# A state-space layer's outputs in another order of matmuls, and its kernels made four pairs at a time

## The chip, the cores and the metric

One of the eight cores of a Trainium2 chip. The metric is the device time of one execution in microseconds, taken by the hardware profiler; of several runs the median counts.

## What is computed

The reference is four layers in a row on 1024 tokens of width 1024: dilated attention, a grouped state-space layer (S5), and two hybrid layers (short convolution, retention, neighbourhood attention). The change lies in the state-space layer alone:

```python
def s5_scan(u, a_re, a_im, log_dt, b_re, b_im, c_re, c_im, d_skip):
    ...
    a_bar = jnp.exp(A * dt)
    b_bar = ((a_bar - 1.0) / A)[..., None] * Bm
    bu = jnp.einsum('bsgc,gpc->bsgp', uf.astype(jnp.complex64), b_bar)
    ...
    _, states = lax.associative_scan(combine, (a_elems, bu), axis=1)
    y = jnp.einsum('bsgp,gcp->bsgc', states, Cm).real
    y = y + d_skip.astype(f).reshape(SSM_N_GROUPS, SSM_GROUP) * uf
```

There are 64 groups `g` of 16 channels `c`, each with 64 complex states `p`.

## The kernel before

Everything is f32, or f32 split into a high and a low part that are multiplied in three matmuls of 128x512 (`mm3`, L168). These projections fill most of TensorE's (PE's) time. Smaller work is cut into jobs, which a counter of matmuls (`tick`, `pace`) lets in between the projections when the program is written down; after that the compiler's scheduler orders each engine's instructions by its own model of when they are ready.

The state-space layer works on 8 blocks of four pairs of groups (index `k` for the pair, `g` for the group within it; the two groups' states lie on partitions 0 to 63 and 64 to 127). Time is cut into 128 chunks of 8 steps. Within a chunk a short kernel is applied directly; across chunks the states are scanned.

*Tables* (`ssm_setup`, during attention). For each block, `ca` makes the matrix that takes states to outputs, `wj` the one that takes inputs to states, and `kmat` (L798 to L819) the kernel within a chunk: for each of the four pairs two products, for the real and the imaginary part, of a 128x32 operand `u_bd` (both groups of the pair side by side, filled by POOL at L805) with a 128x128 slice of `u_A`. All eight go to partitions 0 to 31 of one PSUM bank, at column 128k (L812). DVE copies them out and adds the skip term on the diagonal (L815, L816), and two DMAs store them.

*The layer itself* (`ssm`, `core`). Each block goes through jobs: `load`; `inject` (L905, inputs to state increments, 64 columns of PE at a time); `demod`, `scan`, `remod` on DVE with help of POOL (L916 to L948), which leave the states `S` as a real and an imaginary tile; `outputs(0)` and `outputs(1)`, one per group; `turn`, which transposes the outputs (L969, L970). `outputs(g)` takes one PSUM tile `T` of a pool of two, and for each pair `k` issues three matmuls that accumulate onto the same 128 columns: inputs by kernel (L956, all 128 partitions as contraction), then real and imaginary states by `ca` (L958, 64 partitions, those of group `g`). ACT then applies gelu to each pair (L963).

`together` (L128) issues a list of matmuls and binds all but the first to be queued behind the first; attention uses it for its last products (L132 is the first matmul of a list, L135 the rest).

An f32 matmul leaves two records each of weight load and matmul in the trace. In a row of PE, `64*128 64x128` means a weight of 64 partitions by 128 columns and a moving operand of 64x128.

Of the kernel before, what the change touches and what calls it, by code (L numbers as in the profile page):

```python
# [75 lines left out]
class Ker:  # L76
# [534 lines left out]
    def ssm_setup(self, p):  # L611
# [14 lines left out]
        def room(tag, shape):  # L626

            return p.tile(shape, F32, name=self.uid(tag), tag=tag, bufs=1)
# [21 lines left out]
        def load():  # L650
# [5 lines left out]
            d = p.tile([32, 32], F32, name="u_d", tag="u_d", bufs=1)  # L656
            nc.sync.dma_start(d, A["s_d"])
            t_["d"] = d
            e = p.tile([32, 16], F32, name="u_eye", tag="u_eye", bufs=1)
            V.tensor_tensor(e, self.ident[0:32, 0:16], self.ident[0:32, 16:32], op=ALU.add)  # L660
            t_["eye"] = e
# [136 lines left out]
        def kmat(b):  # L798

            o = t_["ca"].rearrange("p i n j c -> p i n (j c)")  # L800
            kt = room("u_C", [32, 4, 128])
            for i, bb in enumerate(("br", "bi")):
                for g in range(2):
                    r = slice(64 * g, 64 * g + 64)
                    G.tensor_copy(t_["bd"][r, i, :, 16 * g:16 * g + 16], t_[bb][r, b * 4:b * 4 + 4])  # L805
            dd = p.tile([32, 4, 16], F32, tag="u_dd", name=self.uid("u_dd"), bufs=1)
            V.tensor_tensor(dd, t_["eye"].unsqueeze(1).to_broadcast([32, 4, 16]),
                            t_["d"][:, b * 4:b * 4 + 4].unsqueeze(2).to_broadcast([32, 4, 16]), op=ALU.mult)
            ps = self.pt()
            for k in range(4):  # L810
                for i in range(2):
                    nc.tensor.matmul(ps[0:32, k * 128:(k + 1) * 128], t_["bd"][:, i, k], o[:, i, k, 0:128],  # L812
                                     start=i == 0, stop=i == 1)
            pv = ps[0:32].rearrange("p (k n) -> p k n", n=128)
            V.tensor_copy(kt[:, :, 16:128], pv[:, :, 16:128])  # L815
            V.tensor_tensor(kt[:, :, 0:16], pv[:, :, 0:16], dd, op=ALU.add)  # L816
            kd = self.kd[b].rearrange("(k g) c x -> g c k x", g=2)
            for g in range(2):
                nc.sync.dma_start(kd[g, :, :, 128:256], kt[16 * g:16 * g + 16])  # L819
# [42 lines left out]
    def ssm(self, x_src, x_dst, mod, ctx=None):  # L862
# [5 lines left out]
        with ExitStack() as es:  # L868
# [14 lines left out]
            def core(b):  # L883
# [67 lines left out]
                def outputs(g):  # L951
                    ps = self.pt()
                    r = slice(64 * g, 64 * g + 64)
                    for k in range(4):
                        o = ps[:, k * 128:k * 128 + 128]
                        nc.tensor.matmul(o, L["u"][:, 2 * k + g], L["m"][:, 2 * k + g], start=True, stop=False)  # L956
                        for i in range(2):
                            nc.tensor.matmul(o, L["S"][i][r, k], L["ca"][r, i, k], start=False, stop=i == 1)  # L958
                    if g == 0:
                        L["y"] = p.tile([128, 8, 128], F32, tag="y", name=self.uid("y"), bufs=1)  # L960
                    yo = L["y"].rearrange("p i (k g c) -> p g k i c", g=2, c=16)[:, g]
                    for k in range(4):
                        ACT.activation(yo[:, k], ps[:, k * 128:k * 128 + 128].rearrange("p (i c) -> p i c", c=16),  # L963
                                       AF.Gelu_apprx_tanh)
# [8 lines left out]
                return [load, inject, demod, scan, remod, lambda: outputs(0), lambda: outputs(1),  # L973
# [1013 lines left out]
def extras(inp):  # L1987
# [13 lines left out]
    e["s_d"] = np.ascontiguousarray(inp["ssm_d"][0].reshape(32, 32).T)  # L2001
# [61 lines left out]
```

## Time and profile before

| | us |
|---|---|
| runs: median (lowest, highest) of 3 | 3279.22 (3279.18, 3291.76) |
| profiled execution | 3278.89 |
| its span, first to last instruction | 3276.3 |
| PE busy in the span | 3156.0 |
| mean granted TensorE clock, share of full | 0.988 |

The trace shows each instruction's engine, source line, operands, start and duration. A matmul's duration contains a tail in which the next one already runs, so PE's pace is read from one start to the next. Stretches are given in us from the start of the span: 147 to 415 holds the kernels of all eight blocks (and attention's first part), 1390 to 1615 the layer's blocks.

### The profile page before, as it was taken

The numbers are of one execution on the slowest core, as the hardware profiler recorded it, in microseconds if no ns is written. First come the engines' busy times: TensorE is split into PE (matmuls) and PEld (weight loads), VectorE is DVE, ScalarE is ACT, GpSimd is POOL, SyncE is SP. The second block draws the span as 40 slices with busy tenths as digits, with TensorE's granted clock in tenths as the row PEclk, the third lists the DMA queues.
The fourth block names the chain that finished last, engine by engine and source line by source line (L and its number), as shares of the span: only waits on it lengthen the run. The fifth ranks groups of instructions, "written<-read, shape, count | busy, mean of one in ns | idle before, by whom it ended". The sixth has DMA issues, their size and how long they took to land. (4 is left out here: it accounts for less than half of the span.)

```text
span 3276.3 us, 48205 instructions
## 1 busy us (share of the span) xinstructions
PE 3156.0 (96%) x18340; PEld 2605.9 (80%) x18340; DVE 1931.2 (59%) x4147; ACT 1212.1 (37%) x2498; POOL 589.9 (18%) x769
## 2 busy tenths in 40 slices
PE   7999999999999999999999999999999999999998
PEld 6888787877788787778788888777887888778777
DVE  5565668777866647655544734445457754555455
ACT  4544444444444454322332121134443212234351
POOL 1244402121111101111002122210002212210001
PEclk9999999999999999999999999999999999999999
DMA  4223233333322225555433211132215322133232
GB/s 136 60 71 101 72 94 107 90 94 91 105 70 81 73 82 172 183 157 148 122 122 116 73 52 51 51 103 83 77 58 174 107 65 65 46 98 89 69 115 97
DMA packets 325242, 312.86 MB, mean 95 GB/s; under 512 B 27833, under 2 KB 277396, under 8 KB 325012
## 3 DMA queue, kind: packets, MB, share of 16 engines
q1 hardware_dynamic: 325012, 309.80, 31.2%
q8 instruction: 144, 2.36, 0.3%
q14 instruction: 86, 0.70, 0.1%
HBM read 249.64 MB, written 60.09 MB: 95 GB/s over the span
## 5 line engine op out<-in xcount | busy, mean ns | idle before, releaser
L168 PE MATMUL mm<-aTh,wh 128*128 128x512 f32 (+1 forms) x2704 | 1076.1, 398 | 29.2 <-DVE qk L353 8.2
L168 PE MATMUL mm<-aTl,wh 128*128 128x512 f32 (+1 forms) x2704 | 1073.6, 397 | 0.9 <-DVE aTl L221 0.6
L168 PE MATMUL mm<-aTh,wl 128*128 128x512 f32 (+1 forms) x2704 | 1070.0, 396 | 0.6 <-DVE wl L155 0.6
L168 PEld LDWEIGHTS mm<-aTh,wh 128*128 128x128 f32 x2704 | 513.6, 190 | 137.6 <-issue 6.9
L168 PEld LDWEIGHTS mm<-aTh,wl 128*128 128x128 f32 x2704 | 513.6, 190 | 102.7 <-issue 2.9
L168 PEld LDWEIGHTS mm<-aTl,wh 128*128 128x128 f32 x2704 | 513.4, 190 | 102.0 <-issue 4.8
L155 DVE TENSOR_TENSOR wl<-wr,wh 128x1024 fp32r<-128x1024 f32 x176 | 225.4, 1281 | 191.4 <-ACT wh L154 190.9
L154 ACT ACTIVATE wh<-wr 128x1024 fp32r<-128x1024 f32 x176 | 186.0, 1057 | 381.8 <-PE mm L168 329.5
L414 ACT ACTIVATE sb<-sb,st 128x128 f32<-128x128 f32 (+1 forms) x384 | 170.3, 444 | 268.1 <-DVE st L412 266.9
L168 PE MATMUL mm<-wo,aTh 128*128 128x512 f32 x768 | 240.9, 395 | 6.5 <-DVE ys L1964 3.2
L412 DVE CUSTOM_DVE_ANT_0 sb<-S,bt 128x128 f32<-128x128 f32 (+1 forms) x384 | 126.5, 343 | 108.2 <-PE T L425 90.0
L1162 DVE SCALAR_TENSOR_TENSOR ma<-mw,cact,ma 128x256 f32<-128x256 f32 x336 | 179.8, 544 | 15.3 <-DMA mw<-in_w_mod 9.0
L168 PEld LDWEIGHTS mm<-wo,aTh 128*128 128x128 f32 x768 | 143.4, 189 | 37.1 <-DVE ys L1964 3.6
L168 PE MATMUL mm<-wo,aTl 128*128 128x512 f32 x384 | 151.0, 393 | 0.8 <-DVE aTl L1909 0.8
L1726 ACT ACTIVATE nsb<-nsb,nmn 128x640 f32<-128x640 f32 (+1 forms) x108 | 85.6, 793 | 118.0 <-DVE nmn L1723 105.7
L1169 POOL TENSOR_TENSOR ms<-ma,ms 128x256 fp32r<-128x256 f32 x48 | 43.0, 896 | 461.1 <-ACT ms L1168 298.2
L357 POOL CAST qk<-kz 64x512 fp32r<-64x512 f32 x64 | 69.1, 1079 | 212.6 <-ACT kz L351 210.4
L425 PE MATMUL T<-ident,sb 128*128 128x128 f32 x560 | 99.8, 281 | 5.4 <-DVE mr L1173 4.0
L168 PE MATMUL mm<-cTh,wl 128*128 128x256 f32 x352 | 101.7, 289 | 0.6 <-DVE wl L155 0.6
L168 PE MATMUL mm<-cTl,wh 128*128 128x256 f32 x352 | 101.9, 289 | 0.0
L168 PE MATMUL mm<-cTh,wh 128*128 128x256 f32 x352 | 101.4, 288 | 0.0
L1719 DVE CUSTOM_DVE_ANT_0 nsb<-S,zero 128x256 f32<-128x256 f32 x108 | 45.0, 421 | 81.5 <-PE T L1757 29.2
(437 smaller groups left out, 5282.6 us busy)
## 6 DMA issues: line engine op xcount, KB each, us to landing
wr<-in_attn_w_in SPq DMA_DIRECT2D x80, 512.0 KB
wr<-in_w_in SPq DMA_DIRECT2D x64, 512.0 KB
mw<-in_w_mod SPq DMA_DIRECT2D x48, 512.0 KB
tab<-in_c_rpb SPq DMA_DIRECT2D x72, 192.0 KB
Wb<-wgd SPq DMA_DIRECT2D x96, 128.0 KB
x<-x SPq DMA_DIRECT2D x24, 512.0 KB
x<-in_x SPq DMA_DIRECT2D x16, 512.0 KB
wr<-in_ssm_w_in SPq DMA_DIRECT2D x16, 512.0 KB
```

Source lines behind the costliest of these rows:

```text
L154: nc.scalar.activation(h, raw, AF.Copy)
L155: nc.vector.tensor_tensor(l, raw, h.bitcast(F32), op=ALU.subtract)
L168: nc.tensor.matmul(out, s_, m_, start=first and i == 0, stop=last and i == len(todo) - 1)
L357: nc.gpsimd.tensor_copy(at(t[o], g, hf), at(h_[r], g, hf))
L412: nc.vector.tensor_tensor_reduce(out=sb[:, :N], in0=sp[:, a * 256:a * 256 + N], in1=b, scale=1.0, scalar=3e38, op0=ALU.add, op1=ALU.min, a ...
L414: nc.scalar.activation(sb[:, :N], sb[:, :N], AF.Exp, bias=mc, scale=-1.0, accum_out=st[:, 1, g, a, n:n + 1])
L425: nc.tensor.transpose(t[:, c:c + 128], Ps[a][:, b * 128:b * 128 + 128], self.ident)
L1162: V.scalar_tensor_tensor(a, L[h][:, k], c, a, op0=ALU.mult, op1=ALU.add)
L1169: nc.gpsimd.tensor_tensor(l_, L["a", i], h.bitcast(F32), op=ALU.subtract)
L1719: V.tensor_tensor_reduce(out=sb[:, 0:256], in0=C, in1=zero.to_broadcast([128, 256]), scale=-0.125, scalar=3e38, op0=ALU.add, op1=ALU.min, ...
L1726: ACT.activation(sb[:, :n], sb[:, :n], AF.Exp, bias=mc, scale=-1.0, accum_out=den)
```

## The change

`outputs` becomes one job for both groups. It takes both PSUM tiles, issues first the four input products of each group, then all 16 state products in one list, the group (and with it the half of the partitions and the PSUM tile) changing with every matmul. The gelus of both groups follow. Only the first matmul of a bank is marked as its start, and the last as its end. `kmat` writes the four pairs to partitions 32k to 32k+31 of the same 128 columns, in one list that goes over the pairs for the real part and then for the imaginary one; the copy, the skip term and the store take 128 partitions at a time, and the skip vector and the diagonal are laid out to match.

```diff
--- before.py
+++ after.py
@@ -653,12 +653,8 @@
             nc.sync.dma_start(T("cc", [2, 8]), A["c_cc"])
             ACT.activation(self.cact, t_["cc"], AF.Silu)
             nc.sync.dma_start(T("j9", [9]), A["c_j9"])
-            d = p.tile([32, 32], F32, name="u_d", tag="u_d", bufs=1)
-            nc.sync.dma_start(d, A["s_d"])
-            t_["d"] = d
-            e = p.tile([32, 16], F32, name="u_eye", tag="u_eye", bufs=1)
-            V.tensor_tensor(e, self.ident[0:32, 0:16], self.ident[0:32, 16:32], op=ALU.add)
-            t_["eye"] = e
+            nc.sync.dma_start(T("d", [8]), A["s_d"])
+            V.tensor_reduce(T("eye", [16]), self.ident.rearrange("p (g c) -> p c g", c=16), axis=AX.X, op=ALU.add)
             G.memset(T("bd", [2, 4, 32]), 0.0)
             z = room("u_C", [128, 128])
             G.memset(z, 0.0)
@@ -798,25 +794,19 @@
         def kmat(b):
 
             o = t_["ca"].rearrange("p i n j c -> p i n (j c)")
-            kt = room("u_C", [32, 4, 128])
+            kt = room("u_C", [128, 128])
             for i, bb in enumerate(("br", "bi")):
                 for g in range(2):
                     r = slice(64 * g, 64 * g + 64)
                     G.tensor_copy(t_["bd"][r, i, :, 16 * g:16 * g + 16], t_[bb][r, b * 4:b * 4 + 4])
-            dd = p.tile([32, 4, 16], F32, tag="u_dd", name=self.uid("u_dd"), bufs=1)
-            V.tensor_tensor(dd, t_["eye"].unsqueeze(1).to_broadcast([32, 4, 16]),
-                            t_["d"][:, b * 4:b * 4 + 4].unsqueeze(2).to_broadcast([32, 4, 16]), op=ALU.mult)
+            dd = p.tile([128, 16], F32, tag="u_dd", name=self.uid("u_dd"), bufs=1)
+            V.tensor_scalar(dd, t_["eye"], t_["d"][:, b:b + 1], None, op0=ALU.mult)
             ps = self.pt()
-            for k in range(4):
-                for i in range(2):
-                    nc.tensor.matmul(ps[0:32, k * 128:(k + 1) * 128], t_["bd"][:, i, k], o[:, i, k, 0:128],
-                                     start=i == 0, stop=i == 1)
-            pv = ps[0:32].rearrange("p (k n) -> p k n", n=128)
-            V.tensor_copy(kt[:, :, 16:128], pv[:, :, 16:128])
-            V.tensor_tensor(kt[:, :, 0:16], pv[:, :, 0:16], dd, op=ALU.add)
-            kd = self.kd[b].rearrange("(k g) c x -> g c k x", g=2)
-            for g in range(2):
-                nc.sync.dma_start(kd[g, :, :, 128:256], kt[16 * g:16 * g + 16])
+            self.together([(ps[32 * k:32 * k + 32, 0:128], t_["bd"][:, i, k], o[:, i, k, 0:128], i == 0, i == 1)
+                           for i in range(2) for k in range(4)])
+            V.tensor_copy(kt[:, 16:128], ps[:, 16:128])
+            V.tensor_tensor(kt[:, 0:16], ps[:, 0:16], dd, op=ALU.add)
+            nc.sync.dma_start(self.kd[b].rearrange("g c x -> (g c) x")[:, 128:256], kt)
 
         out = [load, base, angle, powers, inputs]
         for b in range(8):
@@ -948,20 +938,21 @@
                     V.tensor_tensor(Si, t2, Si, op=ALU.add)
                     L["S"] = S
 
-                def outputs(g):
-                    ps = self.pt()
-                    r = slice(64 * g, 64 * g + 64)
-                    for k in range(4):
-                        o = ps[:, k * 128:k * 128 + 128]
-                        nc.tensor.matmul(o, L["u"][:, 2 * k + g], L["m"][:, 2 * k + g], start=True, stop=False)
-                        for i in range(2):
-                            nc.tensor.matmul(o, L["S"][i][r, k], L["ca"][r, i, k], start=False, stop=i == 1)
-                    if g == 0:
-                        L["y"] = p.tile([128, 8, 128], F32, tag="y", name=self.uid("y"), bufs=1)
-                    yo = L["y"].rearrange("p i (k g c) -> p g k i c", g=2, c=16)[:, g]
-                    for k in range(4):
-                        ACT.activation(yo[:, k], ps[:, k * 128:k * 128 + 128].rearrange("p (i c) -> p i c", c=16),
-                                       AF.Gelu_apprx_tanh)
+                def outputs():
+
+                    pg = [self.pt() for _ in range(2)]
+                    at = lambda g, k: pg[g][:, k * 128:k * 128 + 128]
+                    for g in range(2):
+                        self.together([(at(g, k), L["u"][:, 2 * k + g], L["m"][:, 2 * k + g], k == 0, False)
+                                       for k in range(4)])
+                    self.together([(at(g, k), L["S"][i][64 * g:64 * g + 64, k], L["ca"][64 * g:64 * g + 64, i, k],
+                                    False, k == 3 and i == 1) for k in range(4) for i in range(2) for g in range(2)])
+                    L["y"] = p.tile([128, 8, 128], F32, tag="y", name=self.uid("y"), bufs=1)
+                    yv = L["y"].rearrange("p i (k g c) -> p g k i c", g=2, c=16)
+                    for g in range(2):
+                        for k in range(4):
+                            ACT.activation(yv[:, g, k], at(g, k).rearrange("p (i c) -> p i c", c=16),
+                                           AF.Gelu_apprx_tanh)
 
                 def turn(hf):
                     ps = self.pt()
@@ -970,7 +961,7 @@
                     V.tensor_copy(gT[:, b].rearrange(nat, i=8)[:, hf * 4:hf * 4 + 4],
                                   ps.rearrange("p (i k) -> p i k", k=128))
 
-                return [load, inject, demod, scan, remod, lambda: outputs(0), lambda: outputs(1),
+                return [load, inject, demod, scan, remod, outputs,
                         lambda: turn(0), lambda: turn(1)]
 
             def gate_tile():
@@ -1998,7 +1989,7 @@
     e["s_b"] = np.ascontiguousarray(np.stack([pairs3(inp["ssm_b_re"][0]), pairs3(inp["ssm_b_im"][0])], 1))
     e["s_c"] = np.ascontiguousarray(np.stack([pairs3(inp["ssm_" + n][0].transpose(0, 2, 1))
                                               for n in ("c_re", "c_im")], 1))
-    e["s_d"] = np.ascontiguousarray(inp["ssm_d"][0].reshape(32, 32).T)
+    e["s_d"] = np.ascontiguousarray(inp["ssm_d"][0].reshape(8, 128).T)
     e["ssm_b_glu_l"] = np.ascontiguousarray(inp["ssm_b_glu"][0].reshape(8, 128).T)
     e["c_k8"] = np.ascontiguousarray(np.broadcast_to(8 * np.arange(128, dtype=np.float32), (128, 128)))
     e["c_cc"] = np.ascontiguousarray(np.stack([inp["c_2"][0].reshape(8, 128).T, inp["c_ctx_2"].reshape(8, 128).T], 1))
```

What the scheduler makes of it, at three places. Line numbers are those of each version; in the new one, all matmuls of `outputs` and `kmat` carry the lines of `together`, L132 and L135.

PE at the first block's kernels, before (`u_bd` is the weight, `u_A` the moving operand, `T` the PSUM tile):

```order
L135 MATMUL O_1424<-PT_1326,V_1180 64x128 x4
L135 MATMUL O_1424<-PT_1383,V_1180 64x128 x2
L812 MATMUL T_1488<-u_A_1339,u_bd 32x128 x8
L168 MATMUL mm_1472<-aTh,wh_1291 128x512
L403 MATMUL S_1509<-qk_120_787,qk_102_654 128x128
```

and now:

```order
L135 MATMUL O_1424<-PT_1326,V_1180 64x128 x4
L135 MATMUL O_1424<-PT_1383,V_1180 64x128 x2
L132 MATMUL T_1488<-u_A_1339,u_bd 32x128
L135 MATMUL T_1488<-u_A_1339,u_bd 32x128 x7
L168 MATMUL mm_1472<-aTh,wh_1291 128x512
```

Here the eight calls stay in one piece at the same place. Of the eight blocks, two were split in the old order (one call, then seven), and one is in the new (four and four). From here on the rows of PE and DVE stand in a somewhat different order in much of attention.

PE in the second block's outputs, before, where group 0 ends and group 1 begins (`T_13537` and `T_13563` are the groups' tiles, `S_13527` and `S_13528` the real and imaginary states):

```order
L956 MATMUL T_13537<-m_13443,u_13444 128x128
L958 MATMUL T_13537<-ca_13439,S_13527 128x128
L958 MATMUL T_13537<-ca_13439,S_13528 128x128
L956 MATMUL T_13563<-m_13443,u_13444 128x128
L958 MATMUL T_13563<-ca_13439,S_13527 128x128
L958 MATMUL T_13563<-ca_13439,S_13528 128x128
```

and now the start of the whole (`T_13537` and `T_13538` the tiles, `S_13519` and `S_13520` the states):

```order
L132 MATMUL T_13537<-m_13435,u_13436 128x128
L135 MATMUL T_13537<-m_13435,u_13436 128x128 x3
L132 MATMUL T_13538<-m_13435,u_13436 128x128
L135 MATMUL T_13538<-m_13435,u_13436 128x128 x3
L132 MATMUL T_13537<-ca_13431,S_13519 128x128
L135 MATMUL T_13538<-ca_13431,S_13519 128x128
L135 MATMUL T_13537<-ca_13431,S_13520 128x128
L135 MATMUL T_13538<-ca_13431,S_13520 128x128
```

The pattern of three repeated eight times; now the last four rows repeat four times, and 25 projection matmuls stand between them and the transposes (23 before). In most other blocks the input products stand some way ahead of the state products, with 13 to 44 projection matmuls between.

DVE in the third block, before (`wl` is the low part of a weight to come, `S_13768` the real and `S_13769` the imaginary states):

```order
L155 TENSOR_TENSOR wl_13844<-wr_13425,wh_13843 128x1024
L944 TENSOR_TENSOR S_13768<-sc_2476_13751,cs_13682 128x4x127
L947 TENSOR_TENSOR S_13769<-sc_2476_13751,cs_13682 128x4x127
L945 TENSOR_TENSOR S_13768<-dt_13766,S_13768 128x4x127
L948 TENSOR_TENSOR S_13769<-dt_2479_13767,S_13769 128x4x127
```

and now (L934 to L938 are the same four instructions):

```order
L934 TENSOR_TENSOR S_13760<-sc_2476_13743,cs_13674 128x4x127
L937 TENSOR_TENSOR S_13761<-sc_2476_13743,cs_13674 128x4x127
L935 TENSOR_TENSOR S_13760<-dt_13758,S_13760 128x4x127
L155 TENSOR_TENSOR wl_13836<-wr_13417,wh_13835 128x1024
L938 TENSOR_TENSOR S_13761<-dt_2479_13759,S_13761 128x4x127
```

The weight's split moved from ahead of the states to between the real and the imaginary ones. On PE, this block's first two state products (of real states) now stand four projection matmuls ahead of the other fourteen.

## Rows read from the trace of the kernel before

**Rows 1.** The page's part 1: busy time, share of the span, instructions of each engine
```profile
PE 3156.0 (96%) x18340; PEld 2605.9 (80%) x18340; DVE 1931.2 (59%) x4147; ACT 1212.1 (37%) x2498; POOL 589.9 (18%) x769
```

**Rows 2.** Table by stretch: us; PE, PEld, DVE, ACT, POOL busy; clock, DMA share, GB/s
```profile
147.00:415.00 268.00, 259.90 (x1534) 215.16 (x1529) 165.94 (x459) 118.89 (x292) 117.30 (x182) 0.99 0.28 82
415.00:1390.00 975.00, 937.32 (x5208) 775.11 (x5208) 678.74 (x1594) 458.57 (x1082) 150.91 (x166) 0.98 0.34 103
1390.00:1615.00 225.00, 224.47 (x1312) 181.32 (x1311) 116.19 (x172) 57.05 (x115) 23.38 (x28) 1.00 0.52 144
```

**Rows 3.** Waits of PE, 1390 to 1616 us: us in total, times, longest
```profile
PE S L905 <- DMA u<-ud: 0.5, 1, 0.5
```

**Rows 4.** Waits of PE, 147 to 415 us
```profile
PE S L403 <- DVE st L412: 5.5, 2, 3.4
PE mm L168 <- DVE qk L353: 2.0, 2, 1.4
```

**Rows 5.** Timeline, transposes of a block: start us, us, engine, instruction, records
```profile
1438.94 1.04 PE L969 MATMUL T<-ident,y 128*128 128x128 f32 x8
```

**Rows 6.** Timeline, one block's injection: its matmuls and their weight loads
```profile
1392.99 1.73 PEld L905 LDWEIGHTS S<-u,wj 128*64 128x64 f32 x32 [0.35 <-issue]
1392.99 1.97 PE L905 MATMUL S<-u,wj 128*64 128x128 f32 x32
```

**Rows 7.** Timeline, retention's scores, row halves in turn into two tiles
```profile
2126.40 1.16 PE L1597 MATMUL S<-qT,kT 64*128 64x128 f32 x16
```

**Rows 8.** Timeline, first block, where the two groups' products touch
```profile
1410.46 0.71 PE L958 MATMUL T<-ca,S 64*128 64x128 f32 x6
```

**Rows 9.** Timeline, PE in the second block's outputs and after
```profile
1425.24 0.38 PE L956 MATMUL T<-m,u 128*128 128x128 f32 x2
...
1426.19 0.49 PE L956 MATMUL T<-m,u 128*128 128x128 f32 x2
1426.61 0.71 PE L958 MATMUL T<-ca,S 64*128 64x128 f32 x4
1427.25 0.49 PE L956 MATMUL T<-m,u 128*128 128x128 f32 x2
...
1433.59 0.50 PE L168 MATMUL mm<-aTl,wh 128*128 128x512 f32 x1
1433.93 0.40 PE L168 MATMUL mm<-aTh,wl 128*128 128x512 f32 x1
1434.16 0.39 PE L168 MATMUL mm<-aTh,wh 128*128 128x512 f32 x1
```

**Rows 10.** Groups by line and shape: records | busy us, mean ns | idle before
```profile
L958 PE MATMUL T<-ca,S 64*128 64x128 f32 x256 | 41.0, 300 | 0.0
```

**Rows 11.** Timeline, first block's kernels and the matmul behind them
```profile
147.27 1.93 PE L812 MATMUL T<-u_A,u_bd 128*32 128x128 f32 x16
149.13 0.50 PE L168 MATMUL mm<-aTh,wh 128*128 128x512 f32 x1
```

**Rows 12.** Timeline, fourth block: injection on PE, then the chain on DVE
```profile
1477.40 1.97 PE L905 MATMUL S<-u,wj 128*64 128x128 f32 x32
...
1479.20 0.69 DVE L916 TENSOR_TENSOR dr<-S,cs 128x512 f32<-128x512 f32 x1 [1.18 <-PE S L905]
...
1489.36 0.68 DVE L948 TENSOR_TENSOR S<-dt,S 128x508 f32<-128x508 f32 x1
1490.24 1.23 DVE L155 TENSOR_TENSOR wl<-wr,wh 128x1024 fp32r<-128x1024 f32 x1 [0.20 <-ACT wh L154]
```

**Rows 13.** Timeline, ACT, last block: table load and one group's gelu
```profile
1602.68 1.28 ACT L963 ACT_TABLE_LOAD   x1 [3.70 <-PE T L958]
1603.97 0.79 ACT L963 ACTIVATE y<-T 128x128 f32<-128x128 f32 x4
```

**Rows 14.** Groups by line and shape, DVE: the kernels' copy
```profile
L815 DVE COPY u_C<-T 32x448 f32<-32x448 f32 x8 | 4.9, 610 | 3.9 <-PE T L812 3.9
```

**Rows 15.** Waits of PE, 415 to 1390 us
```profile
PE S L403 <- DVE st L412: 7.2, 6, 3.5
```

## Prediction

> **What bounds the kernel now.** I read the page first: TensorE is busy for 96% of the span [rows 1], and apart from its own weight loads no engine for over 59%. The table by stretch then separates the two places that the change touches [rows 2]. In 1390 to 1615 us, the stage of the state space, PE is busy for 224.5 of 225 us and DVE for 116. In 147 to 415 us, where attention runs and the state-space tables are made beside it, PE is busy for 259.9 of 268. The waits agree: in the first stretch PE waited once, 0.5 us for a DMA [rows 3]; in the second most of the wait is for attention's softmax on DVE [rows 4]. So a microsecond of PE work taken away in either place should come off the end, unless PE then meets a result that isn't ready. The idle time inside PE is read from starts: durations in the trace include about 0.27 us of tail that the next matmul overlaps.
>
> **What an f32 matmul costs PE.** One call leaves two records. Eight transposes' records take 1.04 us [rows 5]; less the tail, (1.04 - 0.27)/7 = 0.110 us each. The 32 records of the injection, whose neighbours write different column halves, take 1.97 us: (1.97 - 0.27)/31 = 0.055 each [rows 6]. So two halves of the columns do run abreast. For halves of the rows there is a retention stage with the very form wanted here, 64 rows by 128 columns alternating between two PSUM tiles: 16 records in 1.16 us, (1.16 - 0.27)/15 = 0.059, the first change of shape included [rows 7]. A little of it stands in the old order by chance: where the scheduler lets one group's last product touch the other group's first, six records of L958 last as long as four [rows 8].
>
> **The outputs, part one: changes of shape.** The old order alternates input product (128 rows) and two state products (64 rows). One such period takes 1427.25 - 1426.19 = 1.06 us for 2 + 4 records [rows 9]. Six records at 0.110 are 0.66, so the two changes of shape cost 0.40 us. In the order I count 58 unbroken runs of L958 before (8, 8, then seven in each of six blocks); in the new one 10, since the state products of the third and sixth block are split by other matmuls and the rest stand in one piece. 48 runs fewer at 0.40: **19.2 us**.
>
> **Part two: state products abreast.** 256 records [rows 10]. By the pattern of [rows 8] (about 28 pairs over all blocks: the order before has 13 calls too many in its longer runs, two records each) some 56 of them are paired already. The other 200 make 100 pairs, each saving 0.110: **11.0 us**. Lower bound nothing; upper bound the same 11, since a row pair in [rows 7] is no faster than a column pair. I take the whole, because the nearest row has the same shape. The 128 input-product records keep their 0.110.
>
> **The kernels of the table stage.** One block's 16 records stand from 147.27 to 149.13, 1.86 us [rows 11], one after the other at 0.110 since all write partitions 0 to 31. Four abreast they would be four rounds of 0.110 and some 0.12 for the way in and out: 0.56. Eight blocks at 1.30: **10.4 us**. Four groups of columns at once appear nowhere in this trace, so the ends are: two abreast as in [rows 6], eight rounds and 0.12, 1.0 us, 6.9 us in all; none abreast, nothing. I take the four, as the halves already showed no loss. A block is split in each order here and there, which roughly cancels.
>
> The Trainium skill speaks against this part: "TensorE: Matmul & The Clock Gate", Part 3, section "The mechanism", says a weight load overlaps matmuls in flight only when the row group differs, and the four kernels use all the rows. By that rule the 16 loads would stay in line and the part would give about nothing. The trace here disagrees: 32 loads of the injection, all on 128 rows, fit in 1.73 us beside their matmuls [rows 6].
>
> **What waits instead.** (a) In the new order all state products queue behind the first, so PE stands still if the imaginary states are late. After the injection's start at 1477.40 its last record is due 31 x 0.055 later; DVE begins at 1479.20 and the last state is written at 1490.04 [rows 12], 10.9 us after PE let go. The shortest cover in the new order is the seventh block: 16 input records (1.75), 34 projection matmuls at 0.23 (1433.93 to 1434.16 [rows 9]), seven injection calls (0.8), 10.4 in all, 0.5 short. In the third block DVE now has a weight split of 1.23 us [rows 12] between real and imaginary, but 48 projections cover that. In the sixth, two copies and a split stand before the states, again about 0.5 short. I charge **1 us**. (b) The gelus of both groups now follow the products: a table load of 1.28 and two times 0.79 [rows 13], 2.9 us, ahead of the transposes; 25 projections (5.7 us) stand there. Without that cover the 2.9 would be paid eight times. (c) DVE's copy of the kernels, 0.61 us on 32 partitions [rows 14], gets fewer elements per partition; DVE isn't the bound, nothing. SP issues eight stores fewer, off the path. POOL's operand copies wait for these products anyway, and get them earlier; nothing.
>
> **Sum.** 19.2 + 11.0 + 10.4 - 1 = 39.6 us off the profiled execution's 3278.9 gives 3239.3; the median of the runs is 0.3 above that execution, so **3240 us**.
>
> **Rivals.**
> *The new order of attention costs something.* The scheduler reshuffles PE's and DVE's rows from the first kernel block through most of attention. PE is idle there for 8.1 + 37.7 = 46 us [rows 2], in many waits of up to 3.5 us like those on softmax [rows 4, 15]. A third more is 15 us: 3255; a third less, 3225. For: the new rows were placed for a PE that got faster there by 1.3 us at a time, while DVE didn't. Against: nothing in the pieces I compared puts a consumer directly behind its producer. Chance of costing 8 us or more 0.15, of gaining as much 0.05.
> *The kernels gain nothing*, because four narrow products on the same rows have to wait for one another's weights: 3278.9 - 19.2 - 11.0 + 1 = 3249.7, **3250**. Chance 0.10, since [rows 6] shows two of them not waiting. It is what the rule of the Trainium skill's "TensorE: Matmul & The Clock Gate" cited above would give.
> *Neither goes abreast*, because products that accumulate onto a bank hold each other up where [rows 7] wrote once: only the changes of shape go, 3278.9 - 19.2 + 1 = **3261**. Chance 0.04; [rows 8] accumulated too.
> *Slower: PE stands before the state products.* Since they can't be interleaved any more, a DVE chain that is late stops PE itself. To lose the 40.6 and 16 more, each block must wait 7 us; the cover before the states must then be under 4 us, where the order has over 10. At 8 us of wait a block: 3278.9 - 40.6 + 64 = **3302**. Chance 0.03.
> That the change isn't in the program can be excluded: the products do stand in alternation.
>
> **How the numbers follow.** Forecast 0.63, the others as above. The measurement can tell about 0.5%, 16.4 us, from no change. Faster by more takes in the forecast, the gaining order, two thirds of the attention case, the kernels' case and half of the one without pairs: 0.63 + 0.05 + 0.10 + 0.10 + 0.02 = 0.90. Slower: 0.03. Within: the rest, 0.07. The range goes down to 3226, an attention that also waits nearly a third less, and up to 3260, the attention case with the kernels at half; outside are the slower case and the tails.
>
> **What would show it.** Right: L958's successors as 32 records in about 2.0 us, a block's output products in under 4 us instead of 8.35 (1425.24 to 1433.59 in [rows 9]); a kernel block in about 0.6 us; PE waits in the state-space stage of 1 to 2 us; the end of that stage earlier by some 40 us, 10 of them by the end of the tables. Wrong: records at 0.110 in either group, a wait of PE for the last state of several us per block, or a softmax wait grown by more than 10 us in attention.

## The result, and the profile after

| us | before | changed |
|---|---|---|
| runs: median (lowest, highest) of 4 each | 3284.53 (3279.18, 3291.76) | 3250.26 (3242.47, 3254.37) |
| ratio of the changed to before, 95% interval | | 0.9897 [0.9879, 0.9915] |
| profiled execution | 3278.89 | 3247.39 |
| its span | 3276.3 | 3245.4 |

The change takes about 34 us off. A later set of runs on another occasion gave 0.9887 [0.9869, 0.9905] (below). The forecast was 3240 us, or 0.988 of the median it started from, in a range of 3226 to 3260, and "faster by over 0.5%" at 0.90. The measured 3250 is also what one of the rivals gave (the kernels gain nothing). That agreement is a coincidence, as the profile shows at once.

TensorE's busy time fell by 36.2 us; the counts of instructions are those of [rows 1] but for two on ACT:

```profile
PE 3119.8 (96%) x18340; PEld 2576.7 (79%) x18340; DVE 1925.1 (59%) x4147; ACT 1210.5 (37%) x2496; POOL 578.3 (18%) x769
```

To see where the time went I align the two traces by the projections: both programs issue 10800 matmuls into `mm` (L168), and the n-th of one is compared with the n-th of the other. The lead of the changed kernel over before's profiled execution, at the places where before stood at the time given:

| before's time, us | 415 | 1390 | 1500 | 1615 | last projection |
|---|---|---|---|---|---|
| lead of the changed kernel, us | 12.4 | 15.6 | 30.9 | 39.8 | 31.2 |

So 12.4 us come from the table stage, 24.2 from the layer's blocks (39.8 - 15.6), and 8.6 are lost again behind them. Of the 12.4, 1.7 us are the clock's: by there before had lost 3.4 us at the lower of TensorE's two clock levels, the changed kernel 1.7. The 3.2 us between 415 and 1390 are no product's: the lead there changed by between -4.2 and 6.3 us in the kernels below.

**The kernels.** One block's 16 records, PE's timeline, against [rows 11]:

```profile
147.55 0.30 PE L132 MATMUL T<-u_A,u_bd 128*32 128x128 f32 x1
147.56 0.31 PE L135 MATMUL T<-u_A,u_bd 128*32 128x128 f32 x3
147.68 0.27 PE L132 MATMUL T<-u_A,u_bd 128*32 128x128 f32 x1
147.69 0.50 PE L135 MATMUL T<-u_A,u_bd 128*32 128x128 f32 x11
148.12 0.50 PE L168 MATMUL mm<-aTh,wh 128*128 128x512 f32 x1
```

From the first start to the next matmul it is 0.574 us (0.56 forecast, 1.865 before by the same nanoseconds). The records' starts, in ns from the first, stand in four groups of four:

```
0 7 13 20 | 133 140 147 153 | 242 249 256 262 | 352 358 365 372
```

Four products, each 32 columns wide and all on the same 128 rows, start within 20 ns, and a round takes 0.109 us like a single full-width record [rows 5]. DVE's copy of the kernels went from 0.61 us [rows 14] to 0.27.

**The outputs.** The block whose input and state products stand in one piece:

```profile
1404.41 0.38 PE L132 MATMUL T<-m,u 128*128 128x128 f32 x2
...
1406.28 0.37 PE L132 MATMUL T<-ca,S 64*128 64x128 f32 x1
...
1406.50 1.84 PE L135 MATMUL T<-ca,S 64*128 64x128 f32 x29
1408.27 0.50 PE L168 MATMUL mm<-aTl,wh 128*128 128x512 f32 x1
```

The 32 state records take 1408.27 - 1406.28 = 1.99 us (2.0 forecast), two starting 7 ns apart every 0.112 us; the whole is 3.86 us where the second block took 8.35 before [rows 9]. In five other blocks the state products take 1.985 to 2.06 us, and in two they are split in 4 and 28.

**What waits now.** PE's waits in the stretch of the tables, 147 to 415 us, against [rows 4]:

```profile
PE O L132 <- ACT PT L428: 2.8, 4, 0.9
PE mm L168 <- DVE qk L353: 2.6, 3, 2.0
PE T L135 <- POOL u_A L768: 2.2, 1, 2.2
```

The third row is new: in the last block's kernels PE started the four real products and then stood for the imaginary part of `u_A`, which POOL was still to write. POOL's and PE's timelines there:

```profile
389.54 1.53 POOL L518 TENSOR_TENSOR Os<-Os,Wb 128x512 f32<-128x512 f32 x1 [1.97 <-DMA Wb<-wgd]
391.02 1.40 POOL L768 TENSOR_TENSOR u_A<-u_A,u_B 128x576 f32<-128x576 f32 x1
```

```profile
390.03 0.29 PE L135 MATMUL T<-u_A,u_bd 128*32 128x128 f32 x3
392.47 0.56 PE L135 MATMUL T<-u_A,u_bd 128*32 128x128 f32 x8 [2.16 <-POOL u_A L768]
```

The waits in the layer's blocks (1360 to 1580 us of the changed kernel), where [rows 3] had one of 0.5 us:

```profile
PE S L895 <- DMA u<-ud: 4.4, 2, 3.6
PE mm L168 <- ACT ut L983: 1.1, 1, 1.1
PE S L895 <- DMA ca<-cad: 0.6, 1, 0.6
```

(The wait for `ut` lies ahead of the blocks.) No row says that PE waited for the states. What it waited for is the *next* job: the sixth block's injection, whose input `u` comes by DMA. PE's timeline, SP's, and the table by stretch (columns as in [rows 2]; the clock is the last but two):

```profile
1490.45 1.83 PE L135 MATMUL T<-ca,S 64*128 64x128 f32 x29
1495.91 3.24 PE L895 MATMUL S<-u,wj 128*64 128x128 f32 x32 [3.62 <-DMA u<-ud]
1499.08 0.50 PE L168 MATMUL mm<-aTh,wh 128*128 128x512 f32 x1
```

```profile
1483.60 0.38 SPq L984 DMA_DIRECT2D ud<-ut  x1
...
1488.30 5.51 SPq L887 DMA_DIRECT2D u<-ud  x8
```

```profile
1390.00:1495.00 105.00, 100.94 (x672) 84.39 (x670) 59.80 (x87) 30.00 (x67) 11.48 (x18) 1.00 0.62 176
1495.00:1499.00 4.00, 3.09 (x32) 3.02 (x32) 0.03 (x1) 0.12 (x1) 0.00 (x0) 0.57 0.40 124
```

SP issues the eight loads of `u` from 1488.30 to 1493.81, after the store of 1483.60. PE was through with the fifth block's state products at 1492.29 and stood for 3.6 us. At the end of that idle stretch the granted clock is 0.57, most of the four us at 1.2 GHz instead of 2.4, and the injection's 32 records took 3.24 us instead of 1.97 [rows 6]. The wait and what the clock took (1.7 us by the trace's granted clock) make 5.3 us.

Before, PE and then SP. The one wait of [rows 3] was that of the second injection, at 1401.36; the sixth, at 1526.44, had none:

```profile
1401.36 1.97 PE L905 MATMUL S<-u,wj 128*64 128x128 f32 x32 [0.51 <-DMA u<-ud]
...
1519.46 0.71 PE L958 MATMUL T<-ca,S 64*128 64x128 f32 x6
...
1526.44 1.97 PE L905 MATMUL S<-u,wj 128*64 128x128 f32 x32
```

```profile
1512.29 0.34 SPq L993 DMA_DIRECT2D ud<-ut  x1
1517.54 5.64 SPq L897 DMA_DIRECT2D u<-ud  x8
```

While SP issued the sixth block's loads and they landed, PE worked on the fifth block's outputs, from 1519.46 to 1526.44. These 6.98 us are 2.06 now, since the state products go faster and the input products stand further ahead.

**What is lost behind the stage.** The program is the same there, and PE's order too. Summed over the granted clock, before's profiled execution lost 13.6 us there at the lower level, the changed kernel's 23.9: that is the 8.6 us, and somewhat more. The two profiled executions are the ends of a spread: the other ten traces lost 17.1 to 20.5 us there. So the execution on which the prediction stood was a short one: 3278.89 us, where the median of before in the four sets of runs was 3284.53, 3284.86, 3288.68 and 3283.48. That before as a rule loses as much as the others is argued from these medians; only one of its executions has a trace, so it isn't shown that none of the 8.6 us belongs to the change.

### The profile page after: what moved, and what is told of

Same layout as the page of the kernel before. It is cut to its first block, busy times and chain, and to the rows that moved or that the text cites. A ratio compares the mean times of both kernels' runs of the same rounds, so it can differ in the third digit from the quotient of the medians.

```text
span 3245.4 us, 48179 instructions
## 1 busy us (share of the span) xinstructions
PE 3119.8 (96%) x18340; PEld 2576.7 (79%) x18340; DVE 1925.1 (59%) x4147; ACT 1210.5 (37%) x2496; POOL 578.3 (18%) x769
## 5 line engine op out<-in xcount | busy, mean ns | idle before, releaser
L168 PE MATMUL mm<-aTh,wh 128*128 128x512 f32 (+1 forms) x2704 | 1076.6, 398 | 26.6 <-DVE qk L353 9.8
L168 PE MATMUL mm<-aTl,wh 128*128 128x512 f32 (+1 forms) x2704 | 1075.0, 398 | 0.7 <-DVE aTl L221 0.3
L168 PE MATMUL mm<-aTh,wl 128*128 128x512 f32 (+1 forms) x2704 | 1070.1, 396 | 0.8 <-DVE wl L155 0.8
L168 PEld LDWEIGHTS mm<-aTh,wh 128*128 128x128 f32 x2704 | 513.4, 190 | 136.4 <-issue 8.2
L168 PEld LDWEIGHTS mm<-aTh,wl 128*128 128x128 f32 x2704 | 513.2, 190 | 102.6 <-issue 3.7
L168 PEld LDWEIGHTS mm<-aTl,wh 128*128 128x128 f32 x2704 | 513.8, 190 | 100.6 <-issue 5.4
L168 PE MATMUL mm<-wo,aTh 128*128 128x512 f32 x768 | 242.4, 397 | 7.9 <-DVE ys L1955 4.6
L1153 DVE SCALAR_TENSOR_TENSOR ma<-mw,cact,ma 128x256 f32<-128x256 f32 x336 | 174.0, 530 | 15.6 <-DMA mw<-in_w_mod 10.0
L168 PEld LDWEIGHTS mm<-wo,aTh 128*128 128x128 f32 x768 | 144.5, 190 | 38.7 <-DVE ys L1955 5.0
L168 PE MATMUL mm<-wo,aTl 128*128 128x512 f32 x384 | 151.8, 395 | 0.9 <-DVE aTl L1900 0.9
L168 PE MATMUL mm<-cTh,wl 128*128 128x256 f32 x352 | 101.9, 289 | 0.6 <-DVE wl L155 0.6
L168 PE MATMUL mm<-cTl,wh 128*128 128x256 f32 x352 | 102.0, 290 | 0.0
L168 PE MATMUL mm<-cTh,wh 128*128 128x256 f32 x352 | 101.4, 288 | 0.0
```

The source lines that it names most:

```text
L168: nc.tensor.matmul(out, s_, m_, start=first and i == 0, stop=last and i == len(todo) - 1)
L1153: V.scalar_tensor_tensor(a, L[h][:, k], c, a, op0=ALU.mult, op1=ALU.add)
```

## The experiments

| kernel | runs | median us | before, same runs | ratio [95%] | gain 1390 to 1615, us |
|---|---|---|---|---|---|
| changed | 4 | 3250.26 | 3284.53 | 0.9897 [0.9879, 0.9915] | 24.2 |
| changed, again | 6 | 3251.57 | 3288.68 | 0.9887 [0.9869, 0.9905] | 25.2 |
| outputs only | 6 | 3257.94 | 3284.86 | 0.9928 [0.9914, 0.9942] | 23.4 |
| kernels only | 9 | 3270.84 | 3284.86 | 0.9961 [0.9948, 0.9973] | 0.5 |
| groups in turn | 4 | 3251.33 | 3284.86 | 0.9907 [0.9890, 0.9924] | 15.5 |
| pairs in turn | 1 | 3245.12 | | | 24.5 |
| runs of two | 1 | 3251.15 | | | 23.7 |
| runs of four | 1 | 3251.79 | | | 20.3 |
| injection held | 6 | 3245.86 | 3288.68 | 0.9877 [0.9857, 0.9896] | 28.0 |
| injection held, again | 5 | 3246.21 | 3283.48 | 0.9877 [0.9856, 0.9898] | 27.6 |
| both held | 5 | 3243.04 | 3283.48 | 0.9871 [0.9849, 0.9894] | 28.2 |

The last column is the growth of the lead by the count of projections, in the profiled execution. It doesn't contain what the clock does elsewhere, and repeats to 1 us (first two rows; the two of the injection held). The three kernels with one run were made for their traces, and no ratio is given for them.

### One part of the change at a time

*Outputs only*: before, with the new `outputs` and job list alone. *Kernels only*: the changed kernel with the old `outputs(g)` back:

```diff
-                return [load, inject, demod, scan, remod, outputs,
+                return [load, inject, demod, scan, remod, lambda: outputs(0), lambda: outputs(1),
```

> The kernel before with only the outputs changed; the table stage and attention keep their old order. Theory (changes of shape 19 us, row pairs 11 us, a new DMA wait of some 4 us): no difference up to 1390 us, the stage of the state space 25 to 30 us shorter, ratio to the kernel before about 0.991 to 0.993. Rival (the kernels' part gives nothing by the end, since attention's new order takes it back, and the outputs carry the whole gain): ratio about 0.9897 as for the whole change.

> The kernel before with only the kernels four abreast. Theory: a block's kernels take 0.57 us instead of 1.86, the projections are 10 to 12 us ahead at 415 us, and 4 to 10 of that are left at the end of attention and at the end: ratio about 0.997 to 0.998. Rival (attention waits as much longer as the kernels give): ratio 1.000 and waits of PE on attention's softmax and probabilities up by 10 us.

Measured: 0.9928 is 23.7 us off 3284.86 (19 to 28 by the interval), 0.9961 is 12.8 us (9 to 17). Together 36.5, the whole of the change within the intervals. So each part works alone, and neither undoes the other. With the kernels alone attention has its new order and still comes out 12.8 us faster, where the products themselves save 8 x 1.29 = 10.3. Three of the expected figures were missed: the outputs gained 23.4 us in the stage where 25 to 30 were expected, and the kernels alone were 7.5 us ahead at 415 us and 0.9961 at the end, where 10 to 12 and 0.997 to 0.998 were. That execution was 4 us behind before when the stretch of the tables began; in the stretch it gained 11.7. Both of these kernels also show the new waits of their part. *Outputs only*, 1390 to 1616 us:

```profile
PE S L905 <- DMA u<-ud: 5.2, 2, 4.0
```

and *kernels only*, 147 to 420 us:

```profile
PE T L135 <- POOL u_A L768: 2.3, 1, 2.3
```

### Does PE need the alternation?

*Groups in turn* lists all state products of one group, then all of the other; the shape of the run stays:

```diff
-                                    False, k == 3 and i == 1) for k in range(4) for i in range(2) for g in range(2)])
+                                    False, k == 3 and i == 1) for g in range(2) for k in range(4) for i in range(2)])
```

> The changed kernel with the 16 state products listed group after group instead of in alternation; the input products still stand in front, so the changes of shape stay as few. Theory: a block's 32 records take 32 x 0.110 + 0.2 = 3.7 us instead of 1.99, so the stage of the state space is 8 x 1.7 = 14 us longer than in the changed kernel, ratio about 0.994. Rival (only the changes of shape count, PE pairs what it can anyway): 2.0 us a block and ratio 0.990.

PE's timeline of one block:

```profile
1429.94 0.49 PE L132 MATMUL T<-ca,S 64*128 64x128 f32 x2
1430.27 3.17 PE L135 MATMUL T<-ca,S 64*128 64x128 f32 x30
1433.37 0.50 PE L168 MATMUL mm<-aTh,wh 128*128 128x512 f32 x1
```

32 records take 3.43 us (3.20 to 3.43 in the eight blocks) instead of 1.985, and the stage gains 8.7 us less than the changed kernel's (9.7 less than when that ran again). So the alternation is what pairs the halves, and it is worth some 9 of the 24 us; what is left, 15.5, is the changes of shape less the waits. A few records still pair, at the seam between the groups; the expectation, 3.7 us a block, 14 us in the stage and a ratio of 0.994, was too dear. The end of the kernel shows hardly any of it: 0.9907 against 0.9897 is within the intervals, so the stage is the witness here, not the median.

*Pairs in turn* does the same to the kernels, the two products of a quarter of the columns one behind the other:

```diff
-                           for i in range(2) for k in range(4)])
+                           for k in range(4) for i in range(2)])
```

> The changed kernel with the eight kernel products listed pair after pair (real, imaginary, then the next pair) on the same four quarters of the partitions. Theory (it is the turn of the list that brings products abreast, the place alone does not): only the last record of one pair meets the first of the next, 13 rounds of 0.110, some 1.5 us a block. Rival (products for other quarters pass those that wait): 0.57 us as in the changed kernel.

This theory fell. First block:

```profile
153.43 0.30 PE L132 MATMUL T<-u_A,u_bd 128*32 128x128 f32 x1
...
154.03 0.50 PE L168 MATMUL mm<-aTh,wh 128*128 128x512 f32 x1
```

0.597 us instead of 0.574. The records' starts, in ns from the first:

```
0 14 27 40 | 134 148 161 174 | 243 258 270 284 | 353 367 380 395
```

The first call (L132) started at 0, its second record at 134. The second call of the list uses the same quarter and carries a wait of its own in the trace, on the record at 148. The records at 14, 27 and 40 are therefore of calls listed behind it, the third, fifth and seventh: PE lets a matmul for a free part of the array start past waiting ones. That the list kept the order written shows in the fourth block, which the scheduler split: the first call stands alone and the seven others 4.87 us later, as they must if the second call is the first that needs the part of `u_A` written last (in the changed kernel that block is split in four and four). A call that waits for another engine is not passed, though: in the eighth block the second call stood 1.5 us for POOL's `u_A`, and the six behind it stood as well, though three of them need only the real part of `u_A`, which was written, and go to other quarters.

How far does it look past? Two kernels with other runs of the same half, which lie between the changed kernel's (one call) and *groups in turn* (eight):

```diff
-                                    False, k == 3 and i == 1) for k in range(4) for i in range(2) for g in range(2)])
+                                    False, k == 3 and i == 1) for k in range(4) for g in range(2) for i in range(2)])
```

```diff
+                                    False, k == 3 and i == 1) for h in range(2) for g in range(2) for k in (2 * h, 2 * h + 1) for i in range(2)])
```

> The changed kernel with the state products in runs of two calls (real and imaginary of one pair) per half of the rows. Theory (a call is passed by later ones for another part as long as no more than two calls, four records, of its own part stand ahead of them, since runs of two calls did pair in the kernels and a run of eight did not in the outputs): 1.99 us a block, as with strict alternation. Rival (halves of the rows are passed by the last record of a run alone): 32 - 7 = 25 rounds of 0.112 and 0.2, 3.0 us.

> The same with runs of four calls, eight records, per half. Theory (four records of reach): a half's run begins when four records of the other's are left, 20 rounds instead of 16, 2.4 us a block. Rival (the reach is eight records or more): 2.0 us; other rival (last record of a run alone): 32 - 3 = 29 rounds, 3.4 us.

Runs of two, then runs of four:

```profile
1470.85 0.37 PE L132 MATMUL T<-ca,S 64*128 64x128 f32 x1
...
1471.07 1.93 PE L135 MATMUL T<-ca,S 64*128 64x128 f32 x29
1472.93 0.50 PE L168 MATMUL mm<-aTh,wh 128*128 128x512 f32 x1
```

```profile
1469.47 0.49 PE L132 MATMUL T<-ca,S 64*128 64x128 f32 x2
1469.80 2.49 PE L135 MATMUL T<-ca,S 64*128 64x128 f32 x30
1472.22 0.50 PE L168 MATMUL mm<-aTl,wh 128*128 128x512 f32 x1
```

One call, two, four, eight of the same half in a row: 1.985, 2.09, 2.53 to 2.75, 3.20 to 3.43 us in most blocks. Two are nearly as good as one; with four, the other half starts only when three or four records of the first are left, which also explains the seam in *groups in turn*. A waiting list of some four records (two calls) for each part of the array would fit all of these and *pairs in turn*, where a quarter has four records in all; no run measured such a list by itself, and the exact numbers of the expectations were off by 0.1 to 0.35 us.

### The wait for the injection's input

*Injection held*: the changed kernel, with 45 empty jobs ahead of the sixth block's injection, and each injection's loop bound behind the projection that is the last one written down by then, so that the scheduler can't pull it up to the fifth block's state products:

```diff
-            nc.tensor.matmul(out, s_, m_, start=first and i == 0, stop=last and i == len(todo) - 1)
+            self.last = nc.tensor.matmul(out, s_, m_, start=first and i == 0, stop=last and i == len(todo) - 1)
...
+                    with tc.issue_after(self.last.ins):
...
-                return [load, inject, demod, scan, remod, outputs,
+                return [load] + [lambda: None] * (45 if b == 5 else 0) + [inject, demod, scan, remod, outputs,
```

*Changed, again* is the changed kernel as it is, in the same set of runs.

> The changed kernel with the sixth block's injection held behind a later projection matmul, 12 projections (2.7 us) after the fifth block's state products instead of right behind them. Theory (the wait for the input's round trip through memory is the new wait, and the half clock after it follows from it): the 3.6 us wait shrinks to under 1, no stretch of half clock near 1495, the stage ends 4 to 5 us earlier, ratio about 0.0015 below the changed kernel of this call. Rival (the wait moves on to the sixth block's states): PE waits about as long at its state products, ratio unchanged.

> The changed kernel once more. Theory (what was lost after the stage of the state space is half clock that comes and goes between executions, the order there being the same): the lead at 1615 us is about 40 us again, and what is left of it at the end follows the time at half clock behind 1615 us; ratio 0.988 to 0.991. Rival (the loss behind the stage belongs to the change): again 8 us given back at the same places.

Waits of PE for the input, 1360 to 1620 us, injection held:

```profile
PE S L896 <- DMA u<-ud: 1.7, 3, 0.7
```

and the changed kernel again:

```profile
PE S L895 <- DMA u<-ud: 3.5, 1, 3.5
```

The long wait is gone, what remains lies in three short ones, and no stretch at the lower clock stands near it. Over all traces, the clock falls there in each of the seven that have the long wait (2.2 to 4.1 us) and in none of the five others. The stage gains 28.0 us instead of 24.2 and 25.2, and 27.6 when run again: so the wait with its clock cost 2.4 to 3.8 us of the stage, where 4 to 5 were expected. At the end 0.9877 against 0.9887 points the same way, but the intervals overlap.

The changed kernel's second trace missed its own expectation: the lead at 1615 us was 31.7 us, not 40. It was already 5.7 us behind before at 60 us, where PE's order is the same in both programs and the lower clock had taken 6.8 us. Behind the stage it gave back 8.0 us, which is what the rival had said, with 20.5 us lost to the clock against before's 13.6. With the clock's share added back both traces of the changed kernel keep their lead behind 1615 us to within 2 us; whether that share belongs to the change stays open, as said above.

### The wait for POOL

*Both held* keeps the injection held and splits the last kernel block's list: the four imaginary products become a job of their own, behind a later projection (36 rows of PE lie between). *Injection held, again* is in the same set of runs.

```diff
-            self.together([(ps[32 * k:32 * k + 32, 0:128], t_["bd"][:, i, k], o[:, i, k, 0:128], i == 0, i == 1)
-                           for i in range(2) for k in range(4)])
+            def half(i):
+                self.together([(ps[32 * k:32 * k + 32, 0:128], t_["bd"][:, i, k], o[:, i, k, 0:128], i == 0, i == 1)
+                               for k in range(4)])
...
+                with self.tc.issue_after(self.last.ins):
+                    half(1)
```

> The changed kernel with its sixth injection held back behind later projections, and in the last kernel block the four imaginary products made a list of their own, 36 or so rows of PE behind the four real ones. Theory (the 2.2 us wait for POOL in the last kernel block is the list's doing, since it binds the imaginary products to the real ones while POOL has not written them yet): PE waits nowhere for POOL's u_A in 147 to 415 us; the last block's four imaginary products start at once and take 0.3 us or less up to the next matmul; the ratio falls by about 2/3280, 0.0006, against the kernel with the injection held alone, which is at the edge of what the rounds can tell. Rival (the wait belongs to this stretch, where attention's softmax on DVE sets the end): the wait for POOL goes but waits for softmax and DVE in the stretch grow by about as much; the lead at 415 us stays as it was.

> The same kernel as in the run with the injection held, once more, beside the kernel with both held: ratio 0.987 to 0.989, a wait of PE for POOL's u_A of about 2 us in the last kernel block, waits for the injection's input under 2 us in all.

Waits of PE, 147 to 415 us, both held; then injection held, again:

```profile
PE T L425 <- ACT PT L428: 4.0, 1, 4.0
PE mm L168 <- DVE qk L353: 2.6, 3, 2.0
```

```profile
PE O L132 <- ACT PT L428: 2.4, 4, 1.1
PE mm L168 <- DVE qk L353: 2.2, 2, 2.0
PE T L135 <- POOL u_A L768: 2.1, 1, 2.1
```

The wait for POOL is gone, and one of 4.0 us for attention's transposed scores on ACT stands in its place. All PE waits of the stretch add up to 9.0 us with both held and to 8.1 with the one. The lead at 415 us is 11.6 against 12.9, but the lower clock had taken 3.4 us more by then: with that added back (each us at the lower level taken as half a us lost), both held is 2.1 us ahead, just what the wait for POOL had cost. The wait on ACT lies right behind that place, and by 480 us the difference, reckoned in the same way, is 0.2 us. So the 2.2 us were won and given back: in substance the rival was right, attention sets the end of this stretch, on ACT rather than on DVE. The ratios, 0.9871 and 0.9877, can't be told apart. Of all kernels run, this one has the lowest median, 40 us under before's.

## Why the prediction was right, and by what it missed

**Changes of shape and pairs of state products (19.2 + 11.0 us): right.** A block took 3.86 us with both, "under 4" by the forecast. In the stage 28 us came out once the injection was held, and about 1.7 us of wait were left there: 29.7 of 30.2. The runs also part the two: without the alternation 8.7 us are missing, with some records still in pairs at the seam, where 11.0 were forecast for all pairs.

**The kernels four abreast (10.4 us): right**, though nothing in the trace before showed four parts of the array at once. 0.574 us for a block against 0.56; alone, 12.8 us with an interval from 9 to 17. The rival that they gain nothing is out, and so is, for this shape, the rule behind it: "TensorE: Matmul & The Clock Gate" of the Trainium skill, Part 3, "The mechanism", lets a weight load overlap matmuls in flight only on another row group. Four loads on the same 128 rows kept up with a round of 0.109 us. [rows 6] had been the better guide.

**The step that failed is (a) of "What waits instead", the 1 us.** It asked whether DVE would have the states ready, found 10 us of cover, and charged 1 us. That was so: no wait for states stands among PE's waits. But it asked only about the work that the change made, not about what stands behind it. With the fifth block's outputs 4.9 us shorter, PE reached the sixth injection before its input, whose eight loads SP issues after a store; PE stood 3.6 us in one piece, 4.4 in all, with 1.7 us of clock, and taking the long wait away gave the stage 2.4 to 3.8 us back. The waits of 1 to 2 us that the prediction named as its sign were 5.0 in the stage. It had SP down as off the path, and [rows 3] had a warning: the one wait of the stage was already for a transfer of this kind, that of the second injection. In step (b), the gelus' cover held: no wait of PE for `y` is in the stage.

**Attention's new order: costs nothing that can be measured.** PE was idle for 33.8 to 40.5 us between 415 and 1390 in the ten traces with the new order, against 37.7 and 36.8 in the two with the old one. The lead over that stretch varies by 10 us between executions, so a cost of a few us would not show. The new order brought one wait that the prediction didn't name, 2.2 us for POOL, since the list of eight binds the imaginary products to the real ones. Taking it away changed next to nothing by 480 us, because a wait for ACT takes its place. That is the rival's mechanism at a seventh of its price.

**The number.** The ratio forecast was 0.988; 0.9897 and 0.9887 were measured, and 0.9877 with the injection held. Of the 10 us between 3240 and 3250, 5.3 are the base: the prediction added 0.3 us to the profiled execution, as the median of three runs then had it, while the median of four is 3284.53. That the sum was made against an execution that had lost little at the lower clock is no fault of its terms, but three runs spread over 12.6 us had said how little the base was worth. Of the other 5, the wait for the input with its clock explains 2.4 to 3.8; the rest is within what executions differ by. With the injection held the ratio of 0.9877 is 40.4 us (34 to 47 by the interval), against 40.6 for the three terms without the charge. That the profiled execution was 39.8 us ahead at the end of the stage, where the prediction named some 40, is luck: the stage gave 24.2 of the 29.2 us forecast for it, and the tables and attention before it 5 more than forecast. The same kernel's other trace had 31.7 there.

## What to carry to other kernels

Small matmuls that leave part of TensorE's array empty are worth putting side by side, on halves of the rows or on quarters of the columns, and runs of one shape worth keeping together: here about 0.11 us a round whatever was abreast, and some 0.40 us for each run that went. After such a gain look at the job that PE reaches *next*, and at the queue that brings its input: a transfer for which PE hadn't waited at all held it up for 3.6 us. A saving of one per cent is read better from the stage, aligned by work that both kernels share, than from medians that spread over 12 us.

## What the runs showed of the hardware

- Four products on different quarters of the columns, all on the same rows, start 7 ns apart and take one round of 0.109 us; two on halves of the rows 0.112 us.
- PE starts a matmul for a free part of the array past others that wait for theirs: the seventh call at 40 ns, the second at 148. The Trainium skill, "TensorE: Matmul & The Clock Gate", Part 3, "The mechanism", says that matmuls start strictly in the order of the program; the trace of *pairs in turn* disagrees. A call that waits for another engine's result was not passed: six stood 1.5 us behind it.
- It looks past only so far: runs of two calls cost 5% more than alternation, runs of four 28 to 38%, runs of eight 61 to 73%.
- An idle stretch of 3.6 us on PE was followed by a granted clock of 0.57 over four us, and in that time 32 records took 3.24 us instead of 1.97. The drop was there in seven of seven traces with such a wait at this place, and in none of five without.
